# Low parts of weight blocks on GpSimd in the two DeltaNet stages of a four-layer backbone

## The chip, the core and the metric

The kernel runs on one core of a Trainium2 chip. The metric is the device time of one execution in microseconds (us). Five engines work side by side, each through its own queue in a fixed order: TensorE (PE, its weight loads PEld), VectorE (DVE), ScalarE (ACT), GpSimd (POOL) and SyncE (SP), which issues DMAs. An instruction at the head of a queue waits for semaphores, and whatever stands behind it on that engine waits with it. POOL issues DMAs too.

## The reference

Two streams of 256 tokens (context and latent) pass through four layers of width 1024. A layer is a token mixer and a squared-ReLU MLP, each followed by a layer norm. Layers 0 and 3 use the bidirectional gated DeltaNet, layer 1 differential attention, layer 2 an mLSTM. What the DeltaNet mixer computes, cut to its core:

```python
p = hh @ w_in                                    # q, k, v, z and the gates
qkv = silu(centred_dwconv(p[..., :CONV_CH_A], conv_w))
q, k = l2_normalize(q) * DK_A ** -0.5, l2_normalize(k)
g = cumsum(g); decay = exp(g_i - g_j) for i >= j
a_mat = strictly_lower((k * beta) @ k.T * decay) # per head, chunk of tokens, direction
u, w = solve(I + a_mat, v * beta), solve(I + a_mat, k * beta * exp(g))
scan over chunks: v_new = u - w @ s; o = qg @ s + qk @ v_new; s = s * g_last + kdec.T @ v_new
y = (rms_norm(o) * silu(z)) @ w_out
```

All of it is float32.

## The kernel before

**Weights.** A float32 product is made of three matmuls: both operands are split into a high part of reduced precision and a low part that holds the rest. `wblock` loads a block of weights (128 x 1024) into `raw`, ACT casts it to the high part (`whi`, L178), and DVE subtracts it to give the low part (`wlo`, L179). `dense` (L190 to L192) then runs, for each of eight slices, high x high, high x low and low x high. There are three buffers of `raw` and two each of `whi` and `wlo`, so the parts of a block can be made while PE works on the block before. Blocks of another kind are kept for two uses (`keep`, names `khi` and `klo`), and blocks of gates have no separate low part.

**The DeltaNet stage** (`gdn`). 33 blocks are projected: k, q, v, z and one of gates. `START_ORDER` sets the order of the first five in layer 0, `JOBS` that of the others. Each projection of q, k or v is followed by a convolution of five taps, four of them on DVE as `scalar_tensor_tensor` (L906), and a SiLU (L910). Beside the projections runs, for each of two groups of four heads, a chain (`gdn_chain`, `gdn_inverse`): POOL loads decay rows (`row`, L1125) and masks them with `affine_select` (L1059), ACT takes their exponential, DVE forms the triangular matrices (`bn`, L1084), ACT packs them (`comp`), and DVE inverts all 32 x 32 blocks at once by 31 steps of a product (`invt`, L953) and a sum (`W`, L955). From the result `T64`/`T32` (L969, L971) PE joins the blocks by small matmuls (`q1`, L991). When both groups are through, a scan over the chunks (`gdn_scan`) ends the stage.

**Order.** The program is written with priorities, and a scheduler lays it out into one fixed order for each engine before the run: it follows the dependencies, the priorities and its own estimates of durations. A change of engine for one operation thus moves other instructions as well. POOL's queue in these stages holds the issues of `row`, `qg`, `qkm` and `z` loads, the `affine_select`s and a few memsets. A decay row that was written to DRAM by SP (`ed`) comes back by a POOL load (L1117), which waits for the write.

Of the kernel before, what the change touches and what calls it, by code (L numbers as in the profile page):

```python
# [10 lines left out]
F32 = mybir.dt.float32  # L11
# [3 lines left out]
ALU = mybir.AluOpType  # L15
# [103 lines left out]
class Net:  # L119
# [35 lines left out]
    def wblock(self, src, keep=False, queue="sync", tag="raw"):  # L155

        nc = self.nc
        gates = isinstance(src, tuple)
        if gates:
            src, = src  # L160
        with self.tc.high_priority(offset=WPRI):
            raw = self.wp.tile([P, 1024], F32, tag=tag, name="raw", bufs={"raw": WRAW, "wm": WM}[tag])
            if queue == "sync":
                self.load(raw, src)
            else:
                getattr(nc, queue).dma_start(out=raw, in_=src)
            if gates:

                hi = self.u("khi")[:, :].bitcast(F32R) if keep else self.wp.tile([P, 1024], F32R, tag="whi", name="whi", bufs=WHL)[:, :]
                nc.scalar.copy(hi, raw)  # L170
                w, h = (t.rearrange("p (k f) -> p k f", k=8)[:, :, 32:64] for t in (raw[:, :], hi))
                nc.vector.tensor_tensor(out=h, in0=w, in1=h.bitcast(F32), op=ALU.subtract)
                return hi, None
            if keep:
                hi, lo = (self.u(n)[:, :].bitcast(F32R) for n in ("khi", "klo"))
            else:
                hi, lo = (self.wp.tile([P, 1024], F32R, tag=n, name=n, bufs=WHL)[:, :] for n in ("whi", "wlo"))
            nc.scalar.copy(hi, raw)  # L178
            self.low = nc.vector.tensor_tensor(out=lo, in0=raw, in1=hi.bitcast(F32), op=ALU.subtract).ins  # L179
        return hi, lo  # L180

    def dense(self, w, act, ps, streams=BOTH):
# [27 lines left out]
    def proj_first(self, srcs, act, streams=BOTH):  # L210

        if self.start:
            return self.proj_start(srcs[:NSTART], act)
        ws = self.ahead
        pss = [self.ps(tag=t) for t in TAGS]

        def run(c, turns):
            for ks, bs in turns:
                for k in range(*ks):
                    for w, ps in list(zip(ws, pss))[slice(*bs)]:  # L220
                        yield from self.passes(w, act, ps, k, c)

        all_ = lambda g: [None for _ in g]
        if len(streams) == 2:
            fill = run(CTX, (((0, 8), (0, NFIRST)),))
            self.beside(self.norm, fill)
            all_(fill)
            all_(self.norm)
            self.chain = None
            all_(run(LAT, TURNS))  # L230
            self.region.close()
        else:
            all_(run(LAT, TURNS))
        return pss
# [77 lines left out]
    def setup(self):  # L312
        nc = self.nc
        self.cons = self.const.tile([P, NCONST], F32, name="cons")
        self.pars = self.const.tile([P, NPAR], F32, name="pars")
        nc.scalar.dma_start(out=self.pars, in_=self.ins["params"])
        nc.scalar.dma_start(out=self.cons, in_=self.ins["consts"])
        c16 = self.par("c", 0, 16)
        th = self.sm("th", 16, 1)
        nc.scalar.activation(th, c16, AF.Tanh, scale=0.5)  # L320
        nc.vector.scalar_tensor_tensor(out=th, in0=th, scalar=1.0, in1=c16, op0=ALU.add, op1=ALU.mult)

        self.sil = self.const.tile([P, 8, 38], F32, name="sil")
        nc.vector.memset(self.sil, 0.0)
        nc.vector.tensor_scalar(out=self.sil[:, :, 6:8], in0=th.rearrange("p (k s) -> p k s", s=2), scalar1=0.5,  # L325
                                scalar2=None, op0=ALU.mult)
        self.sel = self.const.tile([P, 8], F32, name="sel")
        nc.vector.tensor_reduce(out=self.sel, in_=self.cst("ident").rearrange("p (g x) -> p x g", g=4)[:, 0:8], op=ALU.add, axis=AX.X)

        self.two = self.const.tile([P, 32], F32, name="two")  # L330
        i = self.cst("ident")
        nc.vector.tensor_tensor(out=self.two[0:64], in0=i[0:64, 0:32], in1=i[0:64, 32:64], op=ALU.add)
        self.onesd = self.const.tile([P, 128], F32, name="onesd")
        nc.vector.memset(self.onesd, 1.0 / D)
        self.bias = {}
        for v in (LN_EPS, EPS):
            self.bias[v] = self.const.tile([P, 1], F32, name=f"bias{len(self.bias)}")
            nc.vector.memset(self.bias[v], v)

        def scaled(name, src, f):  # L340
            t = self.const.tile([P, src.shape[1]], F32, name=name)
            nc.vector.tensor_scalar(out=t, in0=src, scalar1=f, scalar2=None, op0=ALU.mult)
            return t


        self.lng = scaled("lng", self.par("ln_g", 0, 64), -0.5)
        self.lnag = scaled("lnag", self.par("ln_g", 0, 64), -0.5 * ALPHA)
        self.lnab = scaled("lnab", self.par("ln_b", 0, 64), ALPHA)
        self.convh = scaled("convh", self.par("conv", 0, 240), 0.5)
        self.normh = scaled("normh", self.par("norm_a", 0, 2), 0.5)  # L350
        self.normch = scaled("normch", self.par("norm_c", 0, 8), 0.5)
        self.gsub = scaled("gsub", self.par("subln", 0), 1.0 - LAM_INIT)
        self.mod = {}
        self.rows, self.row_ws, self.silr, self.credit, self.pace, self.row_li = [], [], None, 0.0, 0.0, None
        self.fetched = None
        self.hn = 0
        self.start = None
        self.asked = None
        self.lag = []
        self.region = ExitStack()  # L360
        self.behind = []
        self.chain = None
# [384 lines left out]
    def run(self):  # L747
        self.setup()
        L = self.layers
        act = self.new_h()  # L750
        self.start = L[:1]
        self.todo = [(li, q) for li in L for q in range(ROWBLOCKS.get(li, 0) // 4, 12)][4:]

        for li in ROWMOD:
            for b in range(ROWBLOCKS[li]):
                ss = BOTH if li < L[-1] or b < 16 else (1,)
                self.rows += [(li, b, s, s == ss[0], b % 8 == 7) for s in ss]
        self.row_loads = [(li, b) for li in ROWMOD for b in range(ROWBLOCKS[li])]
        for n, li in enumerate(L):
            last = n == len(L) - 1  # L760
            need = not last
            kind, j = li % 3, li // 3
            streams = BOTH if need else (1,)
            self.mod_tag = MODTAG[kind]
            self.quota = QUOTA[n]
            o = self.mix(kind, j, li, act, need)

            self.fill(len([c for c in self.todo if c[0] == li or need and c[0] == L[n + 1] and c[1] < 4]))
            self.fill(len(self.todo) % 4)
            self.flush()  # L770
            self.load_res(n == 0, streams)
            aff = self.affine(li, 0, li, 3)
            act = self.new_h()
            w = self.ins[("w_out_a", "w_out_b", "w_out_c")[kind]]
            self.out_norm([w[j, b] for b in range(8)], o, li, 2, 0, streams, aff, act,
                          ahead=[self.ins["w1"][li, f] for f in range(NFIRST)])
            nact, spill = None, None
            if not last:
                nact = self.new_h()
                spill = self.dram.tile([P, 8, NT], F32, tag="spill", name="spill")  # L780
            self.mlp(li, act, streams, lambda: None if last else self.affine(li, 1, L[n + 1], 0), nact, spill,
                     () if last else self.heads(L[n + 1] % 3, L[n + 1] // 3)[:NFIRST])
            self.spill = spill
            act = nact
# [1080 lines left out]
```

## Time and profile before

| | |
|---|---|
| runs of the kernel, median (lowest to highest) | 2714.72 us (2713.13 to 2715.88), 3 runs |
| the profiled execution, its own time | 2714.44 us |
| its span, first to last instruction | 2712.6 us |
| PE busy | 2534.0 us (93%) |
| DVE busy | 1753.3 us (65%) |
| ACT busy | 1302.9 us (48%) |
| POOL busy | 149.8 us (6%) |
| DeltaNet stage of layer 0, of layer 3 (about) | 0 to 400 us, 2160 to 2460 us |

Shares are means over stages with different limits, so a stage is read by itself. Times in the rows count from the start of the span. The profile lists instructions under their source line; L179 is the same line in both kernels, lines further down are 1, 2 or 4 higher in the changed one.

### The profile page before, as it was taken

To read this page: it belongs to the slowest core of one execution; us is meant where nothing else is said; L and a number is where in the kernel's file an instruction comes from. 1 tells how busy PE (TensorE), PEld (TensorE's weight loads), DVE (VectorE), ACT (ScalarE), POOL (GpSimd) and SP (SyncE) were. 2 spreads that over 40 slices of the span, in tenths; PEclk is the share of its full clock that TensorE was granted. 3 is DMA by queue.
4 is the path that set the end of the run, shared out by engine and by line. 5 is a ranking of instruction groups with operands and counts; after the bars stand their busy time and mean duration, and the time that the engine had idled before them with its cause. 6 is when DMAs were issued, how large, how long until landed. Compare 5 with 4: busy or idle time off the path is not lost. (4 is left out here: it accounts for less than half of the span.)

```text
span 2712.6 us, 40330 instructions
## 1 busy us (share of the span) xinstructions
PE 2534.0 (93%) x15596; PEld 2106.8 (78%) x15596; DVE 1753.3 (65%) x3697; ACT 1302.9 (48%) x2521; POOL 149.8 (6%) x259
## 2 busy tenths in 40 slices
PE   8998799999999997999999999899999987978998
PEld 5776688878787665887878877787888876778997
DVE  4798767656647566765664545665454789876555
ACT  4545585433245344543324544363234564556654
POOL 0110020000000000000000000000000020011000
PEclk9998899999999998999999999999999988989999
DMA  7575342445441331244543243323333256533454
GB/s 274 193 270 206 110 141 94 133 154 164 162 136 65 134 113 49 94 140 149 169 155 132 71 154 142 101 86 117 132 128 112 92 168 227 199 110 125 129 186 130
DMA packets 106896, 382.90 MB, mean 141 GB/s; under 512 B 12232, under 2 KB 14280, under 8 KB 106704
## 3 DMA queue, kind: packets, MB, share of 16 engines
q1 hardware_dynamic: 80288, 286.30, 30.9%
q0 software_dynamic: 26128, 93.29, 10.5%
q8 instruction: 123, 2.02, 0.3%
q10 hardware_dynamic: 288, 0.73, 0.1%
q14 instruction: 69, 0.57, 0.1%
HBM read 357.12 MB, written 23.15 MB: 140 GB/s over the span
## 5 line engine op out<-in xcount | busy, mean ns | idle before, releaser
L178 ACT CAST whi<-raw 128x1024 fp32r<-128x1024 f32 x360 | 376.4, 1049 | 826.5 <-PE psd L191 772.6
L179 DVE TENSOR_TENSOR wlo<-raw,whi 128x1024 fp32r<-128x1024 f32 x360 | 440.9, 1225 | 315.8 <-ACT whi L178 315.2
L190 PE MATMUL psd<-hh,whi 128*128 128x512 f32 (+1 forms) x1552 | 582.8, 376 | 7.7 <-ACT whi L178 2.6
L192 PE MATMUL psd<-hh,wlo 128*128 128x512 f32 (+1 forms) x1552 | 579.7, 374 | 3.0 <-DVE wlo L179 3.0
L191 PE MATMUL psd<-hl,whi 128*128 128x512 f32 (+1 forms) x1552 | 579.7, 374 | 0.0
L190 PEld LDWEIGHTS psd<-hh,whi 128*128 128x128 f32 x1552 | 295.9, 191 | 65.9 <-issue 7.0
L190 PE MATMUL psd<-u,whi 128*128 128x512 f32 (+1 forms) x928 | 337.7, 364 | 5.8 <-ACT whi L178 5.8
L192 PEld LDWEIGHTS psd<-hh,wlo 128*128 128x128 f32 x1552 | 295.4, 190 | 57.0 <-DVE wlo L179 4.7
L192 PE MATMUL psd<-u,wlo 128*128 128x512 f32 (+1 forms) x928 | 336.6, 364 | 2.3 <-DVE wlo L179 2.1
L191 PEld LDWEIGHTS psd<-hl,whi 128*128 128x128 f32 x1552 | 295.7, 191 | 53.8 <-issue 3.9
L191 PE MATMUL psd<-u,whi 128*128 128x512 f32 (+1 forms) x928 | 336.5, 363 | 0.0
L643 DVE SCALAR_TENSOR_TENSOR xa<-psd,mod,xa 128x256 f32<-128x256 f32 x280 | 125.9, 480 | 220.8 <-PE psd L192 193.2
L190 PEld LDWEIGHTS psd<-u,whi 128*128 128x128 f32 x928 | 174.4, 188 | 41.3 <-ACT whi L178 12.3
L192 PEld LDWEIGHTS psd<-u,wlo 128*128 128x128 f32 x928 | 174.3, 188 | 35.0 <-DVE wlo L179 6.0
L191 PEld LDWEIGHTS psd<-u,whi 128*128 128x128 f32 x928 | 174.4, 188 | 29.5
L457 DVE SCALAR_TENSOR_TENSOR rowp<-wrow,silr 128x1024 bf16<-128x1024 f32 x160 | 192.0, 1219 | 0.1
L296 DVE TENSOR_TENSOR u<-relu,u 128x512 fp32r<-128x512 f32 (+1 forms) x128 | 79.4, 625 | 53.7 <-ACT u L295 53.7
L433 POOL DMA_DIRECT2D wrow<-in_w_mod_rows_dram x80 | 42.6, 532 | 825.0 <-DVE rowp L457 682.2
L906 DVE SCALAR_TENSOR_TENSOR kq<-conv,convh,kq 128x510 f32<-128x510 f32 (+3 forms) x128 | 85.3, 687 | 4.2 <-ACT kq L899 3.7
L240 PE MATMUL psd<-hh,khi 128*128 128x256 f32 (+1 forms) x248 | 74.1, 307 | 3.5 <-ACT hh L527 3.5
L399 PE MATMUL modps<-wm,sil 128*32 128x512 f32 x448 | 64.9, 630 | 12.5 <-DVE sil L325 6.6
L240 PE MATMUL psd<-hl,khi 128*128 128x256 f32 (+1 forms) x248 | 75.6, 306 | 0.1
(403 smaller groups left out, 4453.6 us busy)
## 6 DMA issues: line engine op xcount, KB each, us to landing
raw<-in_w_dram SPq DMA_DIRECT2D x256, 512.0 KB, 3.5
wm<-in_w_mod_dram SPq DMA_DIRECT2D x112, 512.0 KB, 6.8
wrow<-in_w_mod_rows_dram POOLq DMA_DIRECT2D x80, 512.0 KB, 4.4
raw<-in_w_in_a_dram SPq DMA_DIRECT2D x61, 512.0 KB, 4.3
raw<-in_w_qkog_c_dram SPq DMA_DIRECT2D x17, 512.0 KB, 3.6
row<-gcd POOLq DMA_DIRECT2D x16, 512.0 KB, 5.4
raw<-in_w_out_a_dram SPq DMA_DIRECT2D x16, 512.0 KB, 3.6
raw<-in_w_qk_b_dram SPq DMA_DIRECT2D x16, 512.0 KB, 3.6
```

The lines of the kernel that those rows point to most:

```text
L178: nc.scalar.copy(hi, raw)
L179: self.low = nc.vector.tensor_tensor(out=lo, in0=raw, in1=hi.bitcast(F32), op=ALU.subtract).ins
L190: nc.tensor.matmul(ps[:, c], hi[:, s], rh[:, c], start=k == 0, stop=False)
L191: nc.tensor.matmul(ps[:, c], hi[:, s], rl[:, c], start=False, stop=False)
L192: self.mm = nc.tensor.matmul(ps[:, c], lo[:, s], rh[:, c], start=False, stop=k == 7).ins
L240: self.mm = self.nc.tensor.matmul(ps[:, c], lhs[:, c128(k)], rhs[:, c], start=k == 0 and i == 0, stop=k == 7 and i == len(todo) - 1).ins
L296: self.nc.vector.tensor_tensor(out=lo, in0=src, in1=hi.bitcast(F32), op=ALU.subtract)
L399: mm.append(nc.tensor.matmul(self.mps[r:r + 32, :], self.sil[:, 2 * g + i, 6 - 2 * u:38 - 2 * u], ws[g][:, 512 * i:512 * i + 512], start=u ...
L433: self.behind_mm(self.nc.gpsimd.dma_start(out=w, in_=self.ins["w_mod_rows"][ROWMOD.index(li), b]))
L457: nc.vector.scalar_tensor_tensor(out=out, in0=self.row_w, scalar=0.5, in1=self.silr[s], op0=ALU.mult, op1=ALU.mult, accum_out=self.mod[li] ...
L643: i = getattr(self.nc.vector, name)(**k).ins
L906: nc.vector.scalar_tensor_tensor(out=y3[:, :, o], in0=x3[:, :, i], scalar=tap(t), in1=y3[:, :, o], op0=ALU.mult, op1=ALU.add)
```

## The change

In the two DeltaNet stages the subtraction that gives the low part runs on GpSimd instead of VectorE. A flag is set around the mixer's call; blocks that are kept, and blocks made ahead by the stage before, stay on VectorE.

```diff
             nc.scalar.copy(hi, raw)
-            self.low = nc.vector.tensor_tensor(out=lo, in0=raw, in1=hi.bitcast(F32), op=ALU.subtract).ins
+            self.low = (nc.gpsimd if self.pooled and not keep else nc.vector).tensor_tensor(
+                out=lo, in0=raw, in1=hi.bitcast(F32), op=ALU.subtract).ins
...
+        self.pooled = False
...
+            self.pooled = kind == 0
             o = self.mix(kind, j, li, act, need)
+            self.pooled = False
```

Of 360 subtractions into `wlo` 59 change engine; 301 stay. The scheduler lays out all queues anew.

In VectorE's queue at the start of the first inversion of layer 0 stands, before the change (numbers tell buffers of one name apart):

```order
L179 TENSOR_TENSOR wlo_1391<-raw_1388,whi_1390 128x1024
L953 TENSOR_TENSOR invt_1152<-G_1146,W_1149 128x31
L955 TENSOR_TENSOR W_1149<-W_1149,invt_1152 128x31
L953 TENSOR_TENSOR invt_1152<-G_1146,W_1149 128x60
L955 TENSOR_TENSOR W_1149<-W_1149,invt_1152 128x30x2
L953 TENSOR_TENSOR invt_1152<-G_1146,W_1149 128x87
L906 SCALAR_TENSOR_TENSOR kq_470<-conv_1190,convh_98,kq_470 128x2x254
L955 TENSOR_TENSOR W_1149<-W_1149,invt_1152 128x29x3
L906 SCALAR_TENSOR_TENSOR kq_470<-conv_1190,convh_98,kq_470 128x2x255
L953 TENSOR_TENSOR invt_1152<-G_1146,W_1149 128x112
L179 TENSOR_TENSOR wlo_1486<-raw_1483,whi_1485 128x1024
```

The same place in VectorE's queue after the change:

```order
L957 TENSOR_TENSOR invt_1152<-G_1146,W_1149 128x31
L959 TENSOR_TENSOR W_1149<-W_1149,invt_1152 128x31
L957 TENSOR_TENSOR invt_1152<-G_1146,W_1149 128x60
L959 TENSOR_TENSOR W_1149<-W_1149,invt_1152 128x30x2
L957 TENSOR_TENSOR invt_1152<-G_1146,W_1149 128x87
L910 SCALAR_TENSOR_TENSOR kq_470<-conv_1190,convh_98,kq_470 128x2x254
L959 TENSOR_TENSOR W_1149<-W_1149,invt_1152 128x29x3
L910 SCALAR_TENSOR_TENSOR kq_470<-conv_1190,convh_98,kq_470 128x2x255
L957 TENSOR_TENSOR invt_1152<-G_1146,W_1149 128x112
L910 SCALAR_TENSOR_TENSOR kq_470<-conv_1190,convh_98,kq_470 128x2x255
```

The steps of the inversion and the taps of the convolutions remain in their order, and the subtractions between them are gone.

In POOL's queue of layer 0, where the decay rows of the first group come back for the products of q and k (`row`<-`ed`), stands before the change:

```order
L943 MEMSET W_1149 128x1024
L1117 DMA row_1376<-ed_913 128x1024
L1117 DMA row_1471<-ed_1008 128x1024
L1117 DMA row_1545<-ed_1049 128x1024
L944 MEMSET W_1149 128x32
L1117 DMA row_1600<-ed_1136 128x1024
```

and after the change:

```order
L947 MEMSET W_1149 128x1024
L1121 DMA row_1376<-ed_913 128x1024
L1121 DMA row_1471<-ed_1008 128x1024
L1121 DMA row_1545<-ed_1049 128x1024
L179 TENSOR_TENSOR wlo_1332<-raw_1329,whi_1331 128x1024
L948 MEMSET W_1149 128x32
L179 TENSOR_TENSOR wlo_1391<-raw_1388,whi_1390 128x1024
```

The subtraction for block 1332 now stands behind the issue for `row_1545`, and that for block 1391 behind both.

In POOL's queue of layer 3, where the first group's decay rows are masked, stands before the change:

```order
L1125 DMA row_18271<-gcd_18140 128x1024
L1059 AFFINE_SELECT row_18168<-row_18168 128x512 x2
L1059 AFFINE_SELECT row_18271<-row_18271 128x512 x2
L1125 DMA row_18350<-gcd_18140 128x1024
L1059 AFFINE_SELECT row_18350<-row_18350 128x512 x2
L1125 DMA row_18433<-gcd_18140 128x1024
```

and after the change:

```order
L1129 DMA row_18271<-gcd_18140 128x1024
L179 TENSOR_TENSOR wlo_18552<-raw_18549,whi_18551 128x1024
L1063 AFFINE_SELECT row_18168<-row_18168 128x512 x2
L179 TENSOR_TENSOR wlo_18624<-raw_18621,whi_18623 128x1024
L1063 AFFINE_SELECT row_18271<-row_18271 128x512 x2
L1129 DMA row_18350<-gcd_18140 128x1024
L1063 AFFINE_SELECT row_18350<-row_18350 128x512 x2
L179 TENSOR_TENSOR wlo_18667<-raw_18664,whi_18666 128x1024
L1129 DMA row_18433<-gcd_18140 128x1024
```

Each masking, and the load of the fourth row, now has a subtraction in front of it.

## Rows read from the trace of the kernel before

**Rows 1.** Who PE waited for, whole span: total, times, longest

```profile
PE q L991 <- DVE T L969: 25.6, 5, 10.1
```

**Rows 2.** Busy time by window: window, length, PE, PEld, DVE, ACT, POOL, clock

```profile
145.00:198.00 53.00, 52.62 (x287) 41.74 (x288) 51.89 (x115) 19.00 (x29) 5.92 (x9) 1.00 0.68 243
...
240.00:300.00 60.00, 58.02 (x391) 45.70 (x389) 55.26 (x121) 28.33 (x52) 2.56 (x4) 1.00 0.59 204
...
2239.00:2289.00 50.00, 46.65 (x311) 37.61 (x309) 47.68 (x125) 22.12 (x41) 3.28 (x4) 1.00 0.78 278
...
2325.00:2375.00 50.00, 48.34 (x376) 37.86 (x374) 47.90 (x112) 25.50 (x52) 0.00 (x0) 1.00 0.61 216
```

**Rows 3.** The same windows, L179 alone: window, length, DVE busy (count)

```profile
145.00:198.00 53.00, 9.46 (x8) 1.00 0.68 243
240.00:300.00 60.00, 9.71 (x9) 1.00 0.59 204
2239.00:2289.00 50.00, 11.34 (x10) 1.00 0.78 278
2325.00:2375.00 50.00, 8.54 (x7) 1.00 0.61 216
```

**Rows 4.** Groups of instructions, DVE, 145 to 198 us: count, busy us, mean ns

```profile
L906 DVE SCALAR_TENSOR_TENSOR kq<-conv,convh,kq 128x508 f32<-128x508 f32 (+1 forms) x20 | 15.1, 763 | 0.0
L953 DVE TENSOR_TENSOR invt<-G,W 128x31 f32<-128x31 f32 (+15 forms) x31 | 11.1, 357 | 0.6
L955 DVE TENSOR_TENSOR W<-W,invt 128x31 f32<-128x31 f32 (+15 forms) x31 | 11.0, 353 | 0.5
...
L1106 DVE TENSOR_TENSOR row<-row,qk 128x512 f32<-128x512 f32 x8 | 5.1, 678 | 0.0
L910 DVE SCALAR_TENSOR_TENSOR kq<-conv,kq 128x512 f32<-128x512 f32 x5 | 3.4, 681 | 0.0
```

**Rows 5.** Timeline, POOL: start, duration, instructions merged

```profile
114.12 3.34 POOL L1059 TENSOR_SCALAR_AFFINE_SELECT row<-row 128x512 f32<-128x512 f32 x4 [3.70 <-DMA row<-gcd]
...
125.37 1.22 POOL L1059 TENSOR_SCALAR_AFFINE_SELECT row<-row 128x512 f32<-128x512 f32 x2 [6.88 <-DMA row<-gcd]
...
187.60 1.23 POOL L1059 TENSOR_SCALAR_AFFINE_SELECT row<-row 128x512 f32<-128x512 f32 x2
...
2217.25 2.20 POOL L1059 TENSOR_SCALAR_AFFINE_SELECT row<-row 128x512 f32<-128x512 f32 x2 [4.39 <-DMA row<-gcd]
```

**Rows 6.** Timeline, DVE, at the same times

```profile
115.33 0.59 DVE L1084 SCALAR_TENSOR_TENSOR bn<-kk,nb,row 128x128 f32<-128x128 f32 x2
...
124.17 1.23 DVE L179 TENSOR_TENSOR wlo<-raw,whi 128x1024 fp32r<-128x1024 f32 x1 [1.43 <-ACT whi L178]
125.31 0.17 DVE L705 TENSOR_TENSOR krt<-kry 128x16 f32<-128x16 f32 x1
125.52 0.51 DVE L706 TENSOR_TENSOR krt<-krt,krh 128x16 f32<-128x16 f32 x1
...
188.13 0.97 DVE L953 TENSOR_TENSOR invt<-G,W 128x240 f32<-128x240 f32 x1
...
189.58 0.40 DVE L953 TENSOR_TENSOR invt<-G,W 128x231 f32<-128x231 f32 x1
...
2217.28 1.68 DVE L179 TENSOR_TENSOR wlo<-raw,whi 128x1024 fp32r<-128x1024 f32 x1
```

**Rows 7.** Groups of instructions, POOL: count, busy us, mean ns

```profile
L943 POOL MEMSET W<- 128x1024 f32 x4 | 3.8, 951 | 20.5 <-DVE bn L976 10.7 <-DVE bn L1084 9.8
...
L944 POOL MEMSET W<- 128x32 f32 x4 | 0.6, 162 | 0.2
```

**Rows 8.** Timeline, POOL, layer 0: the issue for row_1545, and layer 3: row_18271

```profile
141.27 0.53 POOL L1117 DMA_DIRECT2D row<-ed  x1 [10.35 <-DMA ed<-row]
...
2211.14 1.23 POOL L1059 TENSOR_SCALAR_AFFINE_SELECT row<-row 128x512 f32<-128x512 f32 x2 [0.52 <-DMA row<-gcd]
```

**Rows 9.** Timeline, PE, layer 0: the first use of the low part of block 1332

```profile
137.46 0.39 PE L192 MATMUL psd<-hh,wlo 128*128 128x512 f32 x1
```

## The prediction

> **What bounds the kernel now.** I read PE's waits first, because PE has the longest busy time in the table above. The longest wait by one cause is PE standing at the small matmuls that join the inverted blocks, for VectorE's last copies of the inverse: 25.6 us in five waits [rows 1]. There are four inversions, two in each DeltaNet stage, so the next thing to see is what VectorE does up to each of those waits. The windows that hold the 31 steps of each inversion show VectorE busy for 51.9 of 53, 55.3 of 60, 47.7 of 50 and 47.9 of 50 us, 10.2 us of idle time in 213 us [rows 2]. PE is nearly as full there, 52.6, 58.0, 46.7 and 48.3 us, since projections run beside the inversion. The two are close to balance, and VectorE is the one that ends last: PE runs out of projections it may do and waits for the inverse. In these windows, then, a microsecond added to VectorE's queue is a microsecond on the path, and one taken away is worth something until PE's 25.6 us are used up. Elsewhere in the stages VectorE has slack and the change in its load is worth little.
>
> **What is removed.** 34 of the 59 moved subtractions lie in the four windows: 8, 9, 10 and 7 [rows 3]. One holds VectorE from its own start to the next start, 125.31 - 124.17 = 1.14 us [rows 6]. That is 34 x 1.14 = 38.8 us less for VectorE on the path. The other 25 lie where VectorE is not last; I count them at zero, hidden by its idle time and by PE's projections.
>
> **What is added on VectorE.** The question is whether VectorE runs freely while GpSimd subtracts. The trace holds a test of it. GpSimd's `affine_select` reads SBUF as the subtraction will. While a pair of them runs from 187.60 to 188.83 [rows 5], a step of the inversion that starts at 188.13 takes 0.97 us, and one nearly as large takes 0.40 us soon after [rows 6]. While another pair runs from 125.37, a product of 16 columns takes 0.51 us after one of the same size took 0.17. At 2217.25 a pair of selects meets VectorE's own low part: the pair takes 2.20 us instead of 1.23, and the subtraction 1.68 us instead of 1.23. But at 115.33, in the midst of four selects, two operations with one input in PSUM (`kk`) take 0.59 us together. So VectorE operations that read two tensors from SBUF are held while GpSimd reads SBUF, until about its end, and GpSimd is held by them; operations with one SBUF input are not.
>
> The Trainium skill, "SBUF — State Buffer", section "Who interferes with whom", states this as a rule: a VectorE instruction with two SBUF inputs and a GpSimd instruction that reads SBUF exclude each other for the whole instruction, and the later one waits in full. By that rule the trace agrees: the step at 188.13 lost 0.57 us, about what was left of the select.
>
> How much of VectorE's work in the windows reads two SBUF tensors? In the first, the taps, the two halves of a step and the SiLU's product do (15.1 + 11.1 + 11.0 + 3.4 = 40.6 us), and the largest group that doesn't is 5.1 us [rows 4]. That is 0.89 of 45.7 us; with the small groups and the transposes of the other windows I take 0.86.
>
> How long does GpSimd read? No subtraction on GpSimd is in the trace. Lower end: two selects read as many elements as one of its inputs, in 1.23 us [rows 5]. Upper end: if the two inputs come one after the other, four selects, 2.46 us. The four would count their start four times; a memset of 1024 columns takes 0.951 us and one of 32 columns 0.162 us [rows 7], so a start is about 0.14 us, and three of them off 2.46 leave about 2.05. I add 0.1 for waits behind a VectorE operation in flight and take 2.15 us, nearer the upper row. VectorE then loses 0.86 x 2.15 = 1.85 us for each subtraction, against 1.14 saved: +0.71 us, times 34 = +24 us. Half of the 10.2 us in which VectorE was idle anyway can take some of it: -5. This part comes to +19 us. At the ends it is 34 x (0.86 x 1.23 - 1.14) - 5 = -8 us and, with nothing absorbed and every microsecond lost, 34 x (2.46 - 1.14) = +45 us.
>
> The Trainium skill, "GPSIMD Engine Reference", section "3.1 Elementwise — side-by-side cycle accounting", gives 4497 ns for a two-input operation of 2048 columns on GpSimd; half of it is an estimate of 2.25 us for 1024. No run here shows it yet. By it this part would be +22 us in place of +19.
>
> **What is added in POOL's queue.** The subtraction now stands in line with issues that wait. In layer 0 the low part of block 1332 comes behind the issue for `row_1545`, which left only at 141.27, after 10.35 us for a write to land [rows 8]. With 0.53 us of issue and 2.15 us of subtraction the low part is there at 143.95, and PE read it at 137.46 [rows 9]: 6.5 us late. What hides it is PE's later wait for the inverse; what doesn't is that the convolution of that block stands in VectorE's queue between steps of the inversion. Between 0 and 6.5 I take 4. In layer 3 the second decay row was masked at 2211.14 [rows 8]; its masking now stands behind the subtraction for block 18624, whose inputs were there at 2217.28 [rows 6]. That is up to 6.1 + 2.15 = 8.3 us late for the chain that feeds the inversion, and nothing if that block's cast comes earlier in ACT's new order. I take 4. Elsewhere PE reads a low part several microseconds after it was made, and 1 us more is hidden by the second buffer.
>
> **Sum.** +19 + 4 + 4 = +27 us on the profiled execution's 2714.4 us gives 2741 us. That execution lies 0.3 us under the median of the runs, so no correction is needed.
>
> **Rivals.**
>
> *VectorE is relieved after all (faster).* If the subtraction fetches its inputs in short bursts and VectorE slips in between, 38.8 us leave its queue. The gain ends where PE no longer waits, at 25.6 us [rows 1], and the queue on POOL takes 8 back: 2714.4 - 25.6 + 8 = 2697 us. This decides as soon as VectorE is held for less than 1.14 us by each subtraction. For it: operations with a PSUM input ran on undisturbed, and POOL is nearly empty. Against it: every two-input operation that met a select was held, even one of 16 columns. Chance 0.17.
>
> *It cancels (same).* If GpSimd reads both inputs at the pace of one, 1.23 us, VectorE loses 1.06 us and saves 1.14: -8 us with the idle time, +8 from POOL's queue, 2714 us. Against it: the select that is the measure has a single input. Chance 0.11.
>
> *POOL's queue decides (slower still).* If the late low part and the late masking are covered by nothing (6.5 + 8.3 us), and in each of the two other chains two subtractions in front of a masking cost 2 x 2.15 us, 19 + 14.8 + 8.6 = 42 us are added, 2757 us. For it: in both stages issues, masks and subtractions alternate. Against it: most of the maskings were early by several microseconds. Chance 0.16.
>
> The forecast itself has 0.56. Its own range is 2722 to 2765 us.
>
> **How the numbers follow.** Within 0.2% (5.4 us) of the time before is what a measurement of this kernel can't tell from no change. Faster than that: the first rival (0.17) and a little of the second, 0.19. Same: most of the second and the lowest end of the forecast, 0.10. Slower: the rest, 0.71. The range from 2698 to 2770 leaves out the better half of the first rival and the upper end of the third with the forecast's last extreme (+45 + 15), together under 0.2.
>
> **What would show it.** Right: 59 subtractions on GpSimd of about 2.2 us; in the four inversions the taps and the steps have means well above 0.76 and 0.36 us [rows 4]; the windows from the first step to the last are 4 to 8 us longer each; PE's wait for the copies of the inverse is above 25.6 us; PE waits for a low part near block 1332. Wrong: unchanged means of taps and steps with GpSimd subtracting beside them (first rival), subtractions of 1.3 us or less (second), or long idle times of PE whose releaser is the low part itself (third).

## The result and the profile after

The changed kernel takes 2757.3 us (median, 2753.8 to 2758.5) beside 2715.3 us (2713.1 to 2719.8) for the kernel before on the same chip: ratio 1.015, 95% interval 1.0138 to 1.0162, so 42 us slower, where 27 were forecast. The profiled execution took 2753.8 us, with a span of 2752.0 against 2712.6.

The page of the changed kernel: busy time of each engine, share of the span, instructions.

```profile
PE 2551.2 (93%) x15596; PEld 2117.0 (77%) x15596; DVE 1781.7 (65%) x3638; ACT 1301.2 (47%) x2521; POOL 300.6 (11%) x318
```

VectorE gave up 59 subtractions and is busier than before by 28 us (1753.3 to 1781.7). The groups of instructions say why. First the moved subtractions, whole span (count, busy us, mean ns, idle before):

```profile
L179 POOL TENSOR_TENSOR wlo<-raw,whi 128x1024 fp32r<-128x1024 f32 x59 | 149.4, 2534 | 297.5 <-ACT whi L178 263.8 <-DMA wm<-in_w_mod_dram 12.7 <-PE modps L401 7.1
```

then VectorE's largest groups in the first inversion, 145.3 to 201.1 us, which answer to [rows 4] (the lines have moved by four):

```profile
L910 DVE SCALAR_TENSOR_TENSOR kq<-conv,convh,kq 128x508 f32<-128x508 f32 (+1 forms) x20 | 18.9, 953 | 0.1
L957 DVE TENSOR_TENSOR invt<-G,W 128x31 f32<-128x31 f32 (+15 forms) x31 | 15.0, 483 | 0.7
L959 DVE TENSOR_TENSOR W<-W,invt 128x31 f32<-128x31 f32 (+15 forms) x31 | 14.3, 462 | 0.6
L1110 DVE TENSOR_TENSOR row<-row,qk 128x512 f32<-128x512 f32 x8 | 5.2, 678 | 0.0
```

The same taps and steps have means of 953, 483 and 462 ns where they had 763, 357 and 353. To see the single operations, lay the two engines' timelines together: in 53 of the 59 cases some VectorE operation that starts beside a subtraction ends about where the subtraction does. Its time beyond the lower quartile of its own kind (same line, same shape, same run) I call *held*. Held time comes to 94 us; 59 subtractions moved take 59 x 1.14 = 67 us off VectorE, and the difference, 27 us, is what its busy time grew by (28).

The four inversions, from the first step to the last. [rows 2] has wider windows, so here they are before, cut the same way (window, length, PE, PEld, DVE, ACT, POOL, granted clock of TensorE, share and rate of the DMAs):

```profile
145.90:198.20 52.30, 52.20 (x285) 41.74 (x286) 51.16 (x116) 18.09 (x28) 5.92 (x9) 1.00 0.68 242
240.60:296.50 55.90, 55.90 (x381) 44.28 (x380) 51.19 (x118) 26.21 (x49) 1.80 (x3) 1.00 0.60 207
2238.90:2285.60 46.70, 46.70 (x311) 37.71 (x309) 44.41 (x122) 18.72 (x32) 2.73 (x3) 0.99 0.80 285
2324.80:2372.90 48.10, 47.66 (x373) 37.64 (x372) 46.02 (x112) 23.89 (x49) 0.00 (x0) 1.00 0.63 224
```

and in the changed kernel:

```profile
145.30:201.10 55.80, 53.93 (x278) 42.27 (x278) 54.52 (x107) 18.46 (x29) 19.11 (x12) 0.94 0.59 201
245.70:304.70 59.00, 57.99 (x377) 45.21 (x377) 54.60 (x112) 27.16 (x52) 20.19 (x12) 0.95 0.62 215
2264.60:2314.20 49.60, 46.45 (x292) 37.62 (x292) 48.10 (x111) 17.02 (x29) 20.07 (x10) 0.93 0.63 225
2353.80:2406.90 53.10, 48.50 (x373) 37.68 (x372) 51.80 (x106) 25.52 (x54) 17.64 (x7) 1.00 0.54 194
```

They are 3.5, 3.1, 2.9 and 5.0 us longer, 14.5 together. The granted clock of three of them fell from about 1.00 to 0.93 to 0.95, a mean between its two levels; the fourth kept 1.00 and is longer by the most, so the lower clock is not what lengthens that one. What it adds in the others is not separated here. PE's waits, whole span, answer to [rows 1] (total, times, longest):

```profile
PE q L995 <- DVE T L973: 31.1, 6, 10.9
...
PE kk L1082 <- DVE bn L1088: 12.1, 5, 4.1
...
PE psd L191 <- DVE z L1326: 10.2, 4, 6.2
PE psd L193 <- POOL wlo L179: 6.8, 5, 2.0
```

The wait for the inverse has grown from 25.6 to 31.1. A new one stands beside it: PE waits up to 6.2 us for VectorE to empty a PSUM tile of `z`. For a low part itself PE waits little, never more than 2.0 us, and not near block 1332.

So 14.5 of the 39.4 us of span lie in the inversions. The largest other piece, 13.5 us, lies in layer 3 ahead of its first inversion. The experiments had to say what made that.

### The profile page after: what moved, and what is told of

Its sections match the earlier page's. It is cut to its first block, busy times and chain, and to the rows that moved or that the text cites. A ratio compares the mean times of both kernels' runs of the same rounds, so it can differ in the third digit from the quotient of the medians.

```text
span 2752.0 us, 40324 instructions
## 1 busy us (share of the span) xinstructions
PE 2551.2 (93%) x15596; PEld 2117.0 (77%) x15596; DVE 1781.7 (65%) x3638; ACT 1301.2 (47%) x2521; POOL 300.6 (11%) x318
## 5 line engine op out<-in xcount | busy, mean ns | idle before, releaser
L191 PE MATMUL psd<-hh,whi 128*128 128x512 f32 (+1 forms) x1552 | 587.5, 379 | 18.4 <-DVE z L1326 10.2
L179 DVE TENSOR_TENSOR wlo<-raw,whi 128x1024 fp32r<-128x1024 f32 x301 | 368.1, 1224 | 296.6 <-ACT whi L178 296.1
L179 POOL TENSOR_TENSOR wlo<-raw,whi 128x1024 fp32r<-128x1024 f32 x59 | 149.4, 2534 | 297.5 <-ACT whi L178 263.8
L910 DVE SCALAR_TENSOR_TENSOR kq<-conv,convh,kq 128x510 f32<-128x510 f32 (+3 forms) x128 | 121.3, 963 | 20.7 <-ACT kq L903 19.9
```

What stands on the lines that cost most here:

```text
L179: self.low = (nc.gpsimd if self.pooled and not keep else nc.vector).tensor_tensor(out=lo, in0=raw, in1=hi.bitcast(F32), op=ALU.subtract).ins
L191: nc.tensor.matmul(ps[:, c], hi[:, s], rh[:, c], start=k == 0, stop=False)
L910: nc.vector.scalar_tensor_tensor(out=y3[:, :, o], in0=x3[:, :, i], scalar=tap(t), in1=y3[:, :, o], op0=ALU.mult, op1=ALU.add)
```

## The experiments

Three readings were set against each other: VectorE is held while GpSimd subtracts (H); GpSimd's queue makes other things late (Q); and, once the first runs left something over, the order that the scheduler lays out for the changed kernel costs (R).

**Writing without reading.** GpSimd fills the low part with zeros by three memsets, 2.45 us together, and reads nothing; the product with the low part is thereby left out in the two stages.

```diff
-            nc.scalar.copy(hi, raw)
-            self.low = (nc.gpsimd if self.pooled and not keep else nc.vector).tensor_tensor(
-                out=lo, in0=raw, in1=hi.bitcast(F32), op=ALU.subtract).ins
+            cast = nc.scalar.copy(hi, raw).ins
+            if self.pooled and not keep:
+                parts = [nc.gpsimd.memset(lo[:, c].bitcast(F32), 0.0).ins for c in (slice(0, 1024), slice(0, 1024), slice(0, 512))]
+                self.depend(parts[0], cast, True)
...
```

> Changed kernel, but each of the 59 low parts on GpSimd is filled with zeros by three memsets (1024, 1024 and 512 columns, together about 2.4 us, as long as the subtraction, waiting for the same cast), so the product with the low part of these blocks is left out in value, not in matmuls. GpSimd is as busy and its queue as long, but it reads nothing from SBUF. Theory H (VectorE is held while GpSimd reads SBUF): VectorE is relieved of 34 x 1.14 us in the inversions and held by nothing, so the time falls below the kernel before: 2690 to 2712 us, and the taps are back at a mean of about 0.69 to 0.70 us. Rival Q (what stands in POOL's queue, late low parts and late masks): the queue is the same, so the time stays near 2757 us, at least 2745.

Measured: 2702.4 us, ratio 0.9947 (0.9932 to 0.9962). The inversions are 9.2, 9.8, 7.8 and 6.8 us shorter. In the first, 139.9 to 182.9 us, the steps are a little under [rows 4], and so are the taps, though not as low as the 690 to 700 ns expected:

```profile
L914 DVE SCALAR_TENSOR_TENSOR kq<-conv,convh,kq 128x508 f32<-128x508 f32 (+1 forms) x20 | 14.9, 744 | 0.1
L963 DVE TENSOR_TENSOR W<-W,invt 128x31 f32<-128x31 f32 (+15 forms) x31 | 10.6, 341 | 0.6
L961 DVE TENSOR_TENSOR invt<-G,W 128x31 f32<-128x31 f32 (+15 forms) x31 | 10.6, 340 | 0.6
```

Relieving VectorE does help, and a GpSimd that is busy as long but reads nothing doesn't hold these steps. The gain is all in layer 0 (17.5 us); layer 3 loses 6.5 although its inversions are shorter, and PE waits 8.0 us there for low parts, where it waited 1.4 before.

**Reading without relief.** The kernel before, and GpSimd repeats each of the 59 subtractions into `raw`, whose content isn't used again.

```diff
             self.low = nc.vector.tensor_tensor(out=lo, in0=raw, in1=hi.bitcast(F32), op=ALU.subtract).ins
+            if self.pooled and not keep:
+                nc.gpsimd.tensor_tensor(out=raw, in0=raw, in1=hi.bitcast(F32), op=ALU.subtract)
```

> Kernel before, with all low parts made on VectorE; in addition GpSimd repeats each of the 59 subtractions afterwards, into the raw buffer, where nobody reads the result. No low part is late, VectorE is not relieved, and GpSimd reads as much as in the changed kernel. Theory H: the changed kernel's loss plus the 34 x 1.14 = 39 us that VectorE saved there: 2757 + 39 = about 2795 us, at least 2775. Rival Q: only loads and masks behind the repeated subtractions are late, low parts are not: 2720 to 2740 us.

Measured: 2797.9 us, ratio 1.030 (1.0285 to 1.0316). The four inversions are 45 us longer together.

**Writing without relief.** As the last, with the three memsets into `raw` in place of the subtraction.

```diff
+                for c in (slice(0, 1024), slice(0, 1024), slice(0, 512)):
+                    nc.gpsimd.memset(raw[:, c], 0.0)
```

> As e2_read_too, but GpSimd fills the raw buffer with three memsets of about 2.4 us together in place of the repeated subtraction: the same load on POOL's queue without a read of SBUF. Theory H: 2712 to 2725 us, what the queue alone costs. Rival Q: the same as e2_read_too within 5 us.

Measured: 2729.3 us, ratio 1.0049 (1.0033 to 1.0066), 4 us above theory H's range and 69 below the run before, where rival Q had it within 5. The inversions are 4 us shorter together. Of the 13 us the profile shows 7.5 in the two stages; 5.3 lie in layers 1 and 2, which the edit doesn't touch. Such drifts, -2.7 to +5.3 us, turn up in the profiled executions of several kernels, so a difference of a few us in one stretch of one run isn't read here. By the medians, reading costs 55 us with the relief (2757 less 2702) and 69 without (2798 less 2729). In each of these pairs the two kernels stand in different orders, so some of that may be the order; a pair in one and the same order follows below.

**Which operations are held.** A kernel that computes nothing of the model: 16 operations of one form on VectorE, first alone, then beside one subtraction on GpSimd, for two forms beside a memset too.

```diff
+                    if rep:
+                        nc.gpsimd.tensor_tensor(out=lo, in0=raw, in1=hi, op=ALU.subtract)
+                    for i in range(16):
+                        op(outs[i % 4], i)
```

> A kernel by itself that computes nothing of the model: series of 16 VectorE operations of one kind, first alone, then beside one GpSimd subtraction of 1024 columns, and two series beside a GpSimd memset of 1024 columns. Theory H: beside the subtraction, one operation of a series takes up to 2.4 us more for two SBUF inputs (512 and 16 columns); as 64-column tensor_scalar operations took 2.38 us in the changed kernel, tensor_scalar and copy from SBUF to SBUF are held too; one PSUM input and the transposes run on unchanged; beside the memset two SBUF inputs are not held. Rival (both share the bandwidth of SBUF): every operation of a series takes somewhat longer, none takes 2 us, and the memset slows them as well.

Its timeline (start, us), for each form GpSimd's instruction and the VectorE operation that starts beside it:

```profile
46.24 2.71 POOL L38 TENSOR_TENSOR lo<-raw,hi 128x1024 f32<-128x1024 f32 x1 [45.80 <-DVE raw L36]
46.67 2.83 DVE L25 SCALAR_TENSOR_TENSOR outb<-ina,inb 128x512 f32<-128x512 f32 x1
...
58.03 2.37 POOL L38 TENSOR_TENSOR lo<-raw,hi 128x1024 f32<-128x1024 f32 x1 [9.08 <-DVE outa L26]
...
58.12 2.31 DVE L26 TENSOR_TENSOR ind<-ina,inb 128x16 f32<-128x16 f32 x1
...
61.55 2.35 POOL L38 TENSOR_TENSOR lo<-raw,hi 128x1024 f32<-128x1024 f32 x1 [1.16 <-DVE raw L36]
61.72 0.41 DVE L27 SCALAR_TENSOR_TENSOR outb<-psum,inb 128x256 f32<-128x256 f32 x1
...
66.87 2.34 POOL L38 TENSOR_TENSOR lo<-raw,hi 128x1024 f32<-128x1024 f32 x1 [2.97 <-DVE raw L36]
66.90 2.46 DVE L28 TENSOR_SCALAR outb<-ina 128x256 f32<-128x256 f32 x1
...
72.29 2.34 POOL L38 TENSOR_TENSOR lo<-raw,hi 128x1024 f32<-128x1024 f32 x1 [3.08 <-DVE raw L36]
72.32 2.45 DVE L29 COPY outb<-ina 128x256 f32<-128x256 f32 x1
...
77.70 2.35 POOL L38 TENSOR_TENSOR lo<-raw,hi 128x1024 f32<-128x1024 f32 x1 [3.08 <-DVE raw L36]
78.16 0.66 DVE L30 STREAM_TRANSPOSE outb<-ina 128x512 f32<-128x512 f32 x1
...
87.21 0.95 POOL L43 MEMSET lo<- 128x1024 f32 x1 [7.16 <-DVE lo L42]
87.67 0.68 DVE L25 SCALAR_TENSOR_TENSOR outb<-ina,inb 128x512 f32<-128x512 f32 x1
...
96.86 1.02 POOL L43 MEMSET lo<- 128x1024 f32 x1 [8.69 <-DVE lo L42]
96.92 1.11 DVE L28 TENSOR_SCALAR outb<-ina 128x256 f32<-128x256 f32 x1
```

Alone these take 0.68, 0.17, 0.41, 0.28, 0.28 and 0.67 us. Held until the subtraction ends, large or small: two tensors from SBUF (2.83 for 512 columns, 2.31 for 16), and also `tensor_scalar` and copy, with one (2.46, 2.45). Not held: one input in PSUM, and the transpose. A memset doesn't hold the two-input form; it does hold `tensor_scalar` (1.11).

**One layer at a time.**

```diff
-            self.pooled = kind == 0
+            self.pooled = kind == 0 and need        # the other run: and not need
```

> The low parts on GpSimd in layer 0 alone (30 of the 59). Theory H: as layer 0 of the changed kernel, which ended 11.8 us late: 2716 + 12 = about 2728 us, 2724 to 2732; layer 3 as before, with inversions of 46.6 and 48.1 us. Rival Q (GpSimd's queue, which the writing kernel priced at 2.6 us for layer 0): 2716 to 2720.

> The low parts on GpSimd in layer 3 alone (29 of the 59). Theory H: as layer 3 of the changed kernel, which lost 27 us (39.4 late at its end, 12.2 at its start): 2716 + 27 = about 2743 us, 2738 to 2748. Rival Q (the queue, which the writing kernel priced at 4.8 us for layer 3): 2718 to 2725. Rival B (layer 3 loses more than layer 0 only because it starts late): 2728, as layer 0 alone.

Measured: 2722.8 us (ratio 1.0031, 1.0019 to 1.0043) and 2749.4 us (1.0125, 1.011 to 1.0141). They add: 7 + 34 = 41. Layer 0 alone is 1 us under its range and layer 3 1 us over; Q and B are missed by more. Layer 3 carries most of the loss with about half of the subtractions (29). Its first inversion starts 12.5 us late, counted from the layer's start; in the changed kernel it is 13.5.

**The first 13 of each stage, and the rest.**

```diff
+            self.npool += self.pooled and not keep
+            pool = self.pooled and not keep and self.npool <= 13        # the other run: > 13
```

> Only the first 13 moved low parts of each DeltaNet stage (26 of the 59) are computed on GpSimd, those that fall before the stage's first inversion; the other 33 are on VectorE again. Theory H (VectorE is held for the rest of a subtraction, and the loss lies where the holding falls): in the changed kernel's trace the first inversion starts 0.6 us earlier in layer 0 (145.3 for 145.9) and 13.4 us later in layer 3 than the shift carried into it, so this kernel takes 2716 - 1 + 13 = about 2728 us, 2722 to 2735, and the four inversions last as long as before (52.3, 55.9, 46.6, 48.1 us, each within 1). Rival A (the loss is made by the inversions alone, and what stands ahead of the first is hidden): 2712 to 2718. Rival Q (the decay rows' masking behind a subtraction in GpSimd's queue): also about 2728, but then layer 3's first inversion starts late with the small VectorE operations before it at their old length, 0.17 to 0.19 us.

> The complement of the run before: all moved low parts but the first 13 of each DeltaNet stage (33 of the 59) are computed on GpSimd. Theory H: the four inversions are longer as in the changed kernel (3.5, 3.1, 3.0 and 5.0 us, together 14.6), layer 3's first inversion starts no later than the shift carried into layer 3, and what is left of 42 us after the 13 of the first parts makes about 2716 + 29 = 2745 us, 2738 to 2752. Rival A (all of it from here on): 2754 to 2760. If the two losses do not add to 42 within 6 us, the loss is not local, and theory H lacks something.

Measured: 2742.3 us (1.0097, 1.0079 to 1.0116) and 2745.8 us (1.011, 1.0093 to 1.0126). The second is as expected; the first lost 27 us where 12 were expected, and the two come to 57 in place of 42. With the first 13 alone, two inversions without a subtraction in them are longer than before all the same (by 2.4 and 4.4 us), where each was expected within 1, and the first inversion of layer 3 starts 17 us late. So the loss isn't local, and H lacks something. What it lacks shows when the programs are laid side by side: in the two halves and in the writing and reading kernels VectorE's other instructions stand in an order of their own, though only low parts differ. The kernels with one layer are closer: in the layer that is moved, VectorE's order is the changed kernel's but for 22 places at most, which goes with their losses adding up.

**The order held.** The next four kernels lay the program out once in a throwaway pass and hold every engine to that order in the real one; only the 59 low parts are left free.

```diff
+        written = [i for i in nc.cur_bb.bb.instructions if i.name not in cls.moved]
+        for q in queues or ():
+            for a, b in zip(q, q[1:]):
+                tc.add_manual_dep(written[b], written[a].name, ...NoSync...)
```

> All low parts on VectorE, as before the change, but every engine's other instructions held to the order of the changed kernel. Theory H (VectorE is held while GpSimd subtracts): the order is worth little, 2708 to 2726 us, and the inversions last 46 to 57 us as before. Rival R (the order that the scheduler lays out once it reckons with GpSimd is what costs): most of the 42 us stay, 2740 to 2760 us.

> The 59 low parts on GpSimd, and every engine's other instructions held to the order of before. Theory H: the holding stays, and the order was not laid out for a low part that takes twice as long, so 2750 to 2780 us. Rival R (the new order costs, not the holding): 2700 to 2725 us.

> The changed kernel's order, with three memsets of the low part (2.45 us together) on GpSimd in place of each of the 59 subtractions: it reads nothing from SBUF, and the product of the low parts is left out in these stages. Theory H: the loss is gone and the relief stays, 2690 to 2714 us, as the writing kernel in its own order (2702). Rival R (order) or Q (GpSimd's queue): 2740 to 2760 us, since both are those of the changed kernel.

> The changed kernel's order; the first 13 moved low parts of each stage on GpSimd, the other 33 on VectorE. It asks whether the parts' losses add once the order is the same (in two orders of their own the parts lost 27 and 30 us, 56 where the whole loses 42). Theory H with losses that add: that part as in the changed kernel, 13 us ahead of layer 3's first inversion and about nothing in layer 0, on top of what the order alone gives: 2722 to 2735 us. Rival S (a part alone loses more than its share, whatever the order): 2738 to 2748 us, as in its own order.

Measured: 2735.3 us (1.0063, 1.0045 to 1.0081), 2747.9 us (1.0116, 1.01 to 1.0132), 2708.5 us (0.9968, 0.9957 to 0.998) and 2739.3 us (1.0085, 1.0066 to 1.0103), beside 2716.8 of before. That makes a table of four:

| low parts on | order of before | order of the change |
|---|---|---|
| VectorE | 2716.8 | 2735.3 |
| GpSimd | 2747.9 | 2757.3 |

(The changed kernel was measured at another time than the rest, when the kernel before took 2715.3, so read the differences with it to 1 or 2 us.) The move alone costs 31 us in the old order and 22 in the new; the new order costs 9 with GpSimd and 19 with VectorE. The first run fell between the ranges (9 us above H's, 5 below R's), the second 2 us below H's and 23 above R's: neither is the whole. In the new order the writing kernel is again faster than before, as H had it; the reading, with the same order and a GpSimd as busy, costs 49 us (2757 less 2708). That doesn't clear the order: the memsets, too, lose time in layer 3 outside its inversions (last row below). The fourth run is 4 us above H's range and inside S's, 2738 to 2748. But most of that is the order, which H had put at little: over VectorE in the same order the first 13 cost 4 us, which leaves 18 of the 22 for the other 33, by difference. So S isn't borne out. None of the kernels that compute everything beats the one before.

By stretch, differences to before from the profiled executions (an inversion from its first step to its last). Those of the changed kernel and of the memsets lie 3.5 and 5.6 us under their medians:

| kernel | layer 0 | of it inversions | layer 3 up to its first inversion | its inversions | its rest |
|---|---|---|---|---|---|
| changed | +11.8 | +6.5 | +13.5 | +8.0 | +5.7 |
| GpSimd, old order | +9.1 | +12.1 | +4.7 | +17.2 | -0.3 |
| VectorE, new order | -2.4 | -3.7 | +19.4 | -3.1 | +5.0 |
| memsets, new order | -14.3 | -13.7 | +8.2 | -13.5 | +7.8 |

## Why the prediction was right in kind and short in size

**What bounds.** Right. The stretches that grew are those where VectorE ends last, and relief of the same stretches by the writing kernel took 34 us off the inversions.

**Held, and by how much.** Right in kind, and the step can be read cleanly where the order is that of before. There the windows are, in the kernel with GpSimd in the old order (columns as above):

```profile
147.50:206.80 59.30, 56.04 (x300) 43.41 (x304) 58.10 (x107) 20.18 (x31) 21.74 (x12) 0.97 0.57 210
246.00:307.00 61.00, 59.79 (x396) 47.03 (x394) 54.31 (x111) 28.07 (x52) 22.84 (x14) 1.00 0.63 224
2254.00:2308.00 54.00, 51.10 (x313) 40.76 (x312) 50.19 (x113) 19.05 (x32) 24.44 (x12) 0.94 0.61 215
2345.10:2403.00 57.90, 54.45 (x392) 42.95 (x390) 53.73 (x105) 27.65 (x56) 21.00 (x8) 0.96 0.52 187
```

30 subtractions lie in them and hold VectorE for 55.3 us, 1.84 each; the prediction had 1.85. Busy time says the same: VectorE's grew from 192.8 to 216.3 us although 29 low parts, 29 x 1.14 = 33.1 us, had left it, which makes 56.6, or 1.89 each. The agreement is partly luck. A subtraction takes 2.41 us (median), not 2.15, and the share of it that is held is 0.76, not 0.86; the two errors cancel. The count was 34, for wider windows, where 30 lie in these, and the net growth of VectorE's busy time came out as forecast, 23.5 us for 24.

The windows are 29.3 us longer, however, and not 19. The rest is the term for idle time. The prediction let VectorE's idle time absorb 5 us; instead VectorE is idle for longer, 15.9 us (59.3 - 58.1 and so on) where it was 10.2 in the same windows before. That is 5.7 more in place of 5 less, and these 10.7 us are the whole gap. The longest of these idle moments end with ACT's pieces of a convolution, PE's small matmuls and, for 2.6 us, the load of a decay row. Why they grew is not shown.

In the changed kernel's own order only 26 subtractions fall into the inversions, and VectorE's idle time there falls to 8.5 us; hence 14.5 us and not 29.3.

The Trainium skill's figure ("GPSIMD Engine Reference", section "3.1 Elementwise — side-by-side cycle accounting"), halved to an estimate of 2.25 us, was low as well: 2.41 in the trace.

"Operations with one SBUF input are not held" was wrong. It was read from `kk`, whose other input is in PSUM, and that is the exception. The small kernel shows `tensor_scalar` and copy held like the others. In the changed kernel's layer 3 it hits the gate chain, small operations one after the other:

```profile
2208.21 2.38 DVE L840 TENSOR_SCALAR gse<-gsq 128x64 f32<-128x64 f32 x1
...
2214.52 2.40 DVE L708 TENSOR_TENSOR krt<-krt,krh 128x16 f32<-128x16 f32 x1
```

The first takes 0.19 us undisturbed, the second 0.17. The Trainium skill, "SBUF — State Buffer", section "Who interferes with whom", says this of copies and `tensor_scalar` in their faster modes beside the rule on two inputs, and that of two such instructions the one that issues first blocks the other for its whole length. Trace and page agree; the prediction used half of the section.

**The other 25 at zero.** In the old order nearly right: outside the inversions the two stages of that kernel lose 30.7 - 29.3 = 1.4 us. In the changed kernel 24.9 us lie there (39.4 - 14.5).

**The queue's two places.** The first, block 1332, did not come about. The issue it was to stand behind waits 1.30 us in the new order, not 10.35 [rows 8], and PE's longest wait for any low part is 2.0 us. The second was the right stretch, but most of the delay came by another operation. The second decay row's masking did stand behind its subtraction (2235.05) and came 4.3 us after the first, where it had come 1.7 after: 2.5 us. More was lost on the gate sums' way through DRAM to the first masking, which needs three GpSimd instructions. GpSimd's timeline before:

```profile
2202.62 0.57 POOL L887 DMA_DIRECT2D gcd<-gcr  x1 [35.30 <-ACT gcr L885]
2204.96 1.12 POOL L1125 DMA_DIRECT2D row<-gcd  x2 [1.77 <-PE nps L923]
2209.40 1.22 POOL L1059 TENSOR_SCALAR_AFFINE_SELECT row<-row 128x512 f32<-128x512 f32 x2 [3.33 <-DMA row<-gcd]
```

in the changed kernel:

```profile
2220.82 2.38 POOL L179 TENSOR_TENSOR wlo<-raw,whi 128x1024 fp32r<-128x1024 f32 x1 [3.93 <-ACT whi L178]
2223.13 0.57 POOL L891 DMA_DIRECT2D gcd<-gcr  x1
2223.72 2.41 POOL L179 TENSOR_TENSOR wlo<-raw,whi 128x1024 fp32r<-128x1024 f32 x1
2227.09 1.11 POOL L1129 DMA_DIRECT2D row<-gcd  x2 [0.96 <-DMA gcd<-gcr]
2228.99 2.36 POOL L179 TENSOR_TENSOR wlo<-raw,whi 128x1024 fp32r<-128x1024 f32 x1 [0.78 <-ACT whi L178]
2233.11 1.89 POOL L1063 TENSOR_SCALAR_AFFINE_SELECT row<-row 128x512 f32<-128x512 f32 x2 [1.77 <-DMA row<-gcd]
2235.05 2.38 POOL L179 TENSOR_TENSOR wlo<-raw,whi 128x1024 fp32r<-128x1024 f32 x1
2237.39 1.68 POOL L1063 TENSOR_SCALAR_AFFINE_SELECT row<-row 128x512 f32<-128x512 f32 x2
```

and with the low parts on GpSimd in the old order:

```profile
2218.52 0.56 POOL L894 DMA_DIRECT2D gcd<-gcr  x1 [3.37 <-ACT gcr L892]
2220.60 1.11 POOL L1132 DMA_DIRECT2D row<-gcd  x2 [1.51 <-DMA gcd<-gcr]
2224.40 3.05 POOL L1066 TENSOR_SCALAR_AFFINE_SELECT row<-row 128x512 f32<-128x512 f32 x4 [2.69 <-DMA row<-gcd]
```

VectorE copies the gate sums at 2201.45, 2218.59 and 2217.23. From there to the first masking it is 8.0 us before, 14.5 in the changed kernel and 7.2 in the old order. Three subtractions stand between in the changed kernel and none in the old order. These 7.3 us are near the 9 that the new order costs with GpSimd. How much of them the subtractions make is shown only for the first, at whose end the sums' write to DRAM is issued (2223.13). After the second and the third GpSimd still waits 0.96 and 1.77 us for a load to land; why these loads took longer than in the old order is not shown.

With VectorE the new order costs 19, which is what the same stretch loses, partly in another way: on PE the small matmul that turns the gate sums (`gtp`) stands 22 matmuls behind the sums, where it followed them directly. That run's times: sums copied at 2207.83, turned at 2211.61. Against before it is 6.4 us late at the copy of the sums, 12.2 at the first masking and 19.1 at the inversion's first step. A wait that goes with the new order, whoever makes the low parts, is PE's wait for `z`, here in the run with VectorE:

```profile
PE psd L194 <- DVE z L1329: 12.9, 4, 5.2
```

In layer 3 up to the first inversion two such waits come to 8.5 us with VectorE, 8.0 in the changed kernel and 8.1 with the memsets. In the two kernels in the old order they come to 1.4 and 1.6 us in the whole span. How much of the time they cost was not tried.

**So the weak step** is the sum's assumption that the change acts inside the order of before, with two places priced by hand, and that idle time takes up a part. In that order the mechanism costs 31 us, where the sum had 27: the inversions give 29.3 and not 19, and the rest 1.4 and not 8, so the closeness of the two is luck in part. The new order adds 9. In the changed kernel the loss is spread otherwise than forecast, 14.5 us in the inversions for 19, and 24.9 outside them for 8.

**The signs.** Of what the prediction named as signs of being right, three came: the taps and steps take longer, the subtractions take about what was said (2.41 us for 2.2), and PE's wait for the inverse grew. Two did not: only one of the four windows is 4 to 8 us longer, and PE has no wait for a low part near block 1332.

**The rivals.** Relief and cancelling fell: reading costs 49 to 69 us. "POOL's queue decides" had the time, 2757, by another sum: its two late places made nothing and 2.5 us. The queue and the rest of the new order make about 9 us, and without GpSimd's reading the loss is gone in the same order.

**What stays open.** Single-run stretches drift by some us, so how the changed kernel's other 18 us outside the inversions (24.9 less the 6.5 of the masking) divide is settled in part only: 4.9 come up to the copy of the gate sums in layer 3, with two operations held for 2.2 each, and 3.6 between the last inversion and the last copies of its result, where 1.6 come by two held copies, one beside a memset and one beside a subtraction, and 2.0 by six other copies that the new order puts in front. The first 13 lose 27 us against before in their own order, and 23 in the changed kernel's, of which 19 are that order's with VectorE; which instruction of an order does that was not tried.

## What to carry to other kernels

Before moving an elementwise operation from VectorE to GpSimd, count not its time on VectorE but what VectorE runs beside it: here each moved operation in the inversions freed 1.14 us and held a VectorE instruction for about 1.85. By the small kernel it could pay beside operations with an input in PSUM or transposes; no run tried that. And where a scheduler lays out the order, compare a change in both orders: a good part of a puzzling difference between two variants may be the order alone.

## What the runs showed of the hardware that was not expected

A GpSimd subtraction of 1024 columns takes 2.34 to 2.37 us in the small kernel, 2.71 where a two-input operation of VectorE was under way as it began, and 2.41 (median) in the changed kernel, up to 4.19. It holds one VectorE instruction to its end even if that needs only 0.17 us (2.40 in layer 3's gate chain), so chains of small operations suffer most for their size. `tensor_scalar` and copy are held with a single SBUF input, the first even by a memset, which reads nothing (1.11 us for 0.28), while the same memset leaves the two-input operation at 0.68. An operation with one input in PSUM stays at 0.41 and a transpose at 0.66.
